# Prompt attention by head pairs, the SSD sample states and the sample outputs of cross attention as rows of adjacent products

## The chip, the cores and the metric

The kernel is one step of a hybrid streaming encoder and runs on one core of one Trainium2 chip. TensorE (PE) multiplies matrices and loads their stationary operands (PEld), VectorE (DVE), ScalarE (ACT) and GpSimd (POOL) do the elementwise work, and SyncE (SP) issues most loads. The metric is the device time of one execution in microseconds (us); smaller is better.

## The reference, cut to what matters

One layer computes, for a prompt of 512 tokens and for 8 sample streams of 16 tokens (one tile of 128 tokens), three branches, their merge, a cross attention and a feed-forward part. Three pieces matter here.

```python
def band_attn_prompt(q, k, v, rel_table):        # 8 heads of 64, chunks of 64 tokens
    ...
    s = einsum('bqhd,bkhd->bhqk', qb, kb) * 64 ** -0.5 + bias
    p = softmax(where(valid, s, neg))
    return einsum('bhqk,bkhd->bqhd', p, vb)

def ssd_chunk(h0, x, dt, bm, cm, a_neg):         # 16 heads of 64, 2 groups, state 128
    ...
    y_off = einsum('bign,bgrpn->bigrp', cm, h0g) * exp(ac)[..., None]
    h_new = h0g * exp(a_last)[..., None] + einsum('bjgn,bgrj,bjgrp->bgrpn', bm, exp(a_last - ac), xdt)
    ...

def memory_attn(h, mk, mv, wq, wo):              # 4 heads of 256 over 256 memory rows
    p = softmax(einsum('bqhd,bkhd->bhqk', q, mk) * 256 ** -0.5)
    o = einsum('bhqk,bkhd->bqhd', p, mv)
    return o @ wo
```

The prompt's attention has 4 query tiles of 128 tokens, and tile t sees t + 1 key tiles. For the samples, `y_off` and the cross attention read one state or one memory per stream, so their stationary operands are only 32 columns wide (two streams of 16 tokens, or 32 query columns of one head).

## The kernel before, in words

Everything is single precision. The large products (projections and feed-forward) split both operands into a high and a low part and run three products; the small products of attention and SSD run directly, and the compiler makes two TensorE instructions of each, so that one `mm` call stands as x2 in the profile.

The program is written by Python generators. Large products are "units" (`add`); each step of a unit is some 6 products. The steps of other work (attention, scans) yield a number, the amount of large products that `pump` puts behind that step, so that TensorE has something to do while VectorE and ScalarE work on the step. A tile scheduler then orders the instructions of each engine at build time, and each engine runs its own list strictly in order. PSUM has four buffers of 128x512 with the tag P for all small products (`PP`), and two double ones with the tag D for units (`PD`). Working tiles in SBUF come from a pool of 41 slots (`U`).

The stages that the change touches:

- `attn_prompt` (136 to 262 us in the profile). For 4 head pairs p, 4 query tiles t and 2 heads h: `scores` multiplies 64 rows of q with 64 rows of k (`asp`, half of the array's rows: rows 0 to 63 for the first head of a pair, 64 to 127 for the second), adds a bias, takes the row maximum and the softmax (`ae`). `out` transposes the probabilities (`apt`, copied to `apT`), and multiplies with the values (`apo`, 64 columns, half of the array's columns). The table `SKA = 3` keeps three heads' probabilities between `scores` and `out`.
- `ssd_sample` (680 to 722 and 840 to 882 us, once per group of 8 heads). For 4 pairs q of streams and 2 streams j: transpose the stream's state (`pht`, copied to `hT` by DVE for j = 0 and by ACT for j = 1), multiply with 32 columns of C (`pys`, a quarter of the array's columns, at columns 32 q), and update the state (`pcu`, then `sc` on DVE). The two `pys` tiles hold two of the four P buffers during the whole loop.
- `cross_sample` (1215 to 1312 us). For 8 streams b and 2 key tiles kt: the probabilities of 4 heads (32 columns each) times the stream's values (`xpv`, a quarter of the array's columns per head). The values come in two halves (`xcv`): heads 0 and 1 use the first, heads 2 and 3 the second.

The same scheduler puts other products between products that wait for different things. So the two halves of a stream's values lead to two pairs of `xpv` products with other work between them.

Of the kernel before, what the change touches and what calls it, by code (L numbers as in the profile page):

```python
# [11 lines left out]
ALU = mybir.AluOpType  # L12
# [7 lines left out]
NT = 5            # token tiles: 4 of the prompt, 1 with the 8 x 16 sample tokens  # L20
# [7 lines left out]
NGA, NGB, NGC = 5, 3, 5    # gates of the branches done ahead  # L28
# [4 lines left out]
SEQ = (0, 1, 2, 4, 3)   # tiles of a group's scan  # L33
LQ = 1
SKA = 3           # softmax tiles ahead of their products
MAGIC = float(0x5F3759DF)

NU = 41           # working slots of 128 x 640
NQ = 16           # of 128 x 128
NW = 6            # half weight tiles, and as many for the low parts  # L40
NS = 17           # small slots


class Enc:
# [39 lines left out]
    # Dense products come as units (generators that yield the time their products hold the tensor  # L84
    # engine); the steps of other work yield how much dense work is to be put behind them.
# [3 lines left out]
    def tick(self):  # L89
        """Next step of the work behind every finished product."""  # L90
        self.posts = [p for p in self.posts if next(p[1], self) is not self]
        for name in [n for n in self.ended if all(p[0] != n for p in self.posts)]:
            self.ended.remove(name)
            self.done.add(name)

    def post(self, gen):
        """First step of the work behind a product; the others come with later products."""
        if gen is not None and next(gen, self) is not self:
            self.posts.append((self.units[0][0] if self.units else None, gen))
# [34 lines left out]
    def weave(self, *gens, lead=0):  # L134
        """Steps of the generators in turn, the first one lead steps ahead."""
# [14 lines left out]
    def fmj(self, wk, X, post, m=P, c=0, nm="fm", split=False):  # L150
        """A weight-stationary product and the steps behind it."""
# [16 lines left out]
    def tmj(self, wk, X, cb, tiles=range(NT), nm="tm", t0=0, late=False):  # L168
        """cb(pair, ps[128 tokens, j, 256]): X^T (weights), per pair of token tiles; X starts at tile t0.
        late: the last row block comes after the others of the first two pairs."""  # L170
# [33 lines left out]
    def load2(self, out, in_):  # L204
        """A load that does not queue behind those of the weights."""
        self.nc.sync.dma_start(out, in_)

# [24 lines left out]
    def split(self, h, l, x, eng=None):  # L232
        """x = h + l exactly, both with 12 significant bits."""
        self.act(h, x)
        self.tt(l, x, h.bitcast(F32), ALU.subtract, eng)

    def rsqrt(self, v_in, scale, eps, post=1.0):
        """post / sqrt(v_in * scale + eps), elementwise on a small tile."""
# [18 lines left out]
    def sumsq(self, x, acc):  # L257
        """acc[p] = sum over the free axis of x*x."""
# [5 lines left out]
    def weights(self, w, c0, width, k0, nk, engs=None, loose=False):  # L264
        """Columns c0..c0+width of row blocks k0..k0+nk as [(h, l)] per row block."""
# [46 lines left out]
    def masks(self):  # L312
        nc = self.nc
        self.one = self.ones("one")
        self.mi = self.ones("mi")                             # [k, i] = 1 for k <= i
        self.keep(self.mi, [[1, P]], 0, -1)
        self.ms, blk = self.ones("ms"), self.Q("blk")         # [k, j] = 1 for k > j, within blocks of 16
# [7 lines left out]
        self.blkc = self.C("blkc", [P, 8])                    # [token, b] = 1 in block b  # L325
# [4 lines left out]
    def levels(self):  # L330
        """[j, i] = 1 where i lies in the upper half and j in the lower half of one block of 2s."""
        nc = self.nc
        self.par = self.C("par", [P, 2])                      # parity of the block of 16
        nc.vector.tensor_reduce(self.par, self.blkc.rearrange("p (a c) -> p c a", c=2), axis=AX.X, op=ALU.add)
        # packed: the diagonal blocks of 32 side by side
# [22 lines left out]
    def loads(self):  # L358
        """Loads of the small parameters and the convolutions' states."""
        I = self.I  # L360
        # vectors over features
# [14 lines left out]
        # parameters per head, on all partitions  # L376
# [16 lines left out]
    def params(self):  # L393
        nc = self.nc
        # vectors transposed; conv taps and gate gains come halved
# [35 lines left out]
    def rel_ap(self, h, nq, c0, n):  # L431
        """[nq, n]: bias of query q and key column c0 + c, column 128 being the query tile's first key."""
# [12 lines left out]
    def XT(self, nm):  # L445
        """Feature-major halves of all tokens: [(h, l)] per feature tile."""
# [3 lines left out]
    def token_norm(self, xs):  # L450
        """[128, n]: 1 / rms of the tokens of n tiles, each given as two halves."""
# [7 lines left out]
    def inv_rms(self, ss):  # L459
        """[128, n]: 1 / rms from the parts' sums of squares, [128, parts, n]."""  # L460
# [20 lines left out]
    def norm_tile(self, x, r, g):  # L481
        """Normalized halves of a token tile, transposed to psum: yields (j, psum [128, 4, 128])."""
# [8 lines left out]
    def norm_T(self, x, gain, to, groups=((0, 1), (2, 3), (4,))):  # L491
        """x[t]: two [128, 512] tiles; fills the feature-major halves of all tokens."""
# [63 lines left out]
    def store_conv(self, lt, cols, hist, op, os):  # L556
        """The batch's new states: row (f, token) of the prompt, then (f, stream, token)."""
# [12 lines left out]
    def decays(self, X):  # L570
# [4 lines left out]
        # 24 columns count, 8 more fill up a quarter of the array  # L575
        for c, c0, n in ((0, 3072, 8), (8, 6152, 16), (24, 3080, 8)):
            self.load(raw[:, :, c:c + n], wv[:, :, c0:c0 + n])
        # a quarter of the array for every two row blocks; their sums come with the transposes
# [15 lines left out]
    def decays_post(self, sb):  # L594
# [6 lines left out]
        # beta = sigmoid  # L601
# [3 lines left out]
        # softplus(x) = max(x, 0) + log1p(exp(-|x|)), log1p(e) = 2 atanh(e / (2 + e))  # L605
# [24 lines left out]
        # sums of the decays: up to a token, after a token, whole tile  # L630
# [27 lines left out]
        # the sums up to a token once more, a row per head, to be read by all partitions  # L658
# [6 lines left out]
    def decay(self, out, ts, hs, eng=None):  # L665
        """out[j, i], the sums of the decays up to token i for tiles ts or heads hs, become the decays from
        token j to i, where i >= j (and at most 1 elsewhere)."""
# [8 lines left out]
    def tr5(self, src, cols=None):  # L676
        """src(t) -> [128, 128]; returns two psum tiles, prompt [128, 512] and sample [128, 128]."""
# [7 lines left out]
    def gdn_dense(self, h, X):  # L685
# [7 lines left out]
        def post(kind):  # L693
            f = kind * 4 + h

            def run(ps):
                c = self.silu_conv(ps, "b", f, 3, [self.vc("bcw", i * 12 + f) for i in range(4)], None,
                                   (lt, kind, 3), "bc")
                if kind < 2:
                    # k and q stay as they are: what their l2 norms would scale goes by token  # L700
# [17 lines left out]
                if kind == 0:  # L718
# [3 lines left out]
                    self.stt(sc[:, 0, :], ss[:, NT:], EPS, rk, ALU.add, ALU.mult)       # 1 / rk  # L722
# [23 lines left out]
        for kind in (1, 0, 2):                                # k, q, v  # L746
            f = kind * 4 + h
            yield from self.fmj(lambda: self.weights(w, 1536 + f * P, P, 0, NK), X, post(kind), nm="bps")
        yield from self.fmj(lambda: self.weights(w, 3080 + h * P, P, 0, NK), X, gate, nm="gps")

    def gdn_solve(self, h):
        """Decays, both products with the keys, and the inverse of I + strictly upper part."""
# [11 lines left out]
        # decays between the tokens of a tile, [j, i]  # L764
# [28 lines left out]
        # E = (I + U)^-1 for U = strictly upper part, by doubling the block size; up to 32 on the diagonal  # L793
        # blocks alone, which lie packed side by side
# [24 lines left out]
        for i in range(1, 5):  # L819
            n = NT if i < 4 else 4                            # the sample's blocks are of 16 tokens  # L820
# [8 lines left out]
        # the blocks above the diagonal: -A^-1 B D^-1  # L829
# [34 lines left out]
    def gdn_run(self, h):  # L864
        """Per tile: w = E^T z, outputs and state; then norm over the head and gate."""
# [11 lines left out]
        # z = v - e^gc (k s0), w = E^T z, o = e^gc (q s0) + M^T w, state  # L877
# [60 lines left out]
        # norm over the head, gate, to feature-major halves  # L938
# [45 lines left out]
    def ssd_pre(self, g, t):  # L984
        """Decay matrices of 8 heads, [j, (h, i)], and the scaled inputs of a token tile."""
# [37 lines left out]
        if smp:  # L1023
            # inputs of the state's update in high and low parts, two streams' 32 tokens three times over:
            # (xh, xh, xl) and (bh, bl, bh), so that one pass brings all three products
# [68 lines left out]
    def ssd_sample(self, g, Cc, xs, bs, y, eg):  # L1094
# [5 lines left out]
        # decay of the whole block per (head, p) partition  # L1100
# [12 lines left out]
        pys = [self.PP("pys"), self.PP("pys")]  # L1113
# [6 lines left out]
        fetch(0)  # L1120
        for q in range(4):
# [3 lines left out]
            for j in range(2):  # L1125
# [6 lines left out]
                else:  # L1132
                    nc.vector.tensor_copy(hT, pt)
                yield FCS
# [801 lines left out]
```

## Time and profile before

| | |
|---|---|
| three runs, us | 1836.38, 1836.98, 1841.36 (median 1836.98) |
| span of the profiled execution, us | 1828.0 |
| PE busy | 1727.6 us, 95% of the span |
| DVE, ACT, POOL busy | 47%, 36%, 34% |
| chain of waits | PE 78%, DVE 10%, DMA 5%, ACT 3% |

The page gives no time of the profiled execution beside its span; the span is 9.0 us below the median of the runs. Busy time of PE is not a good measure of a product's cost, since products overlap in the array: the distance from the start of one row of the timeline to the start of the next is, as long as TensorE does not idle. The rows below are read that way.

### The profile page before, as it was taken

The numbers are of one execution on the slowest core, as the hardware profiler recorded it, in microseconds if no ns is written. First come the engines' busy times: TensorE is split into PE (matmuls) and PEld (weight loads), VectorE is DVE, ScalarE is ACT, GpSimd is POOL, SyncE is SP. The second block draws the span as 40 slices with busy tenths as digits, with TensorE's granted clock in tenths as the row PEclk, the third lists the DMA queues.
The fourth block names the chain that finished last, engine by engine and source line by source line (L and its number), as shares of the span: only waits on it lengthen the run. The fifth ranks groups of instructions, "written<-read, shape, count | busy, mean of one in ns | idle before, by whom it ended". The sixth has DMA issues, their size and how long they took to land.

```text
span 1828.0 us, 34046 instructions
## 1 busy us (share of the span) xinstructions
PE 1727.6 (95%) x13705; PEld 1593.3 (87%) x13705; DVE 866.0 (47%) x1778; ACT 652.7 (36%) x1611; POOL 612.5 (34%) x644
## 2 busy tenths in 40 slices
PE   6589999999999999999999899999989999999997
PEld 6587777889888887988989899987689999999997
DVE  5034655255777674665544463342474413431433
ACT  4034444432533442343342255332433312321333
POOL 4151222212332353453333236211144433433433
PEclk9889999999999999999999999999989999999999
DMA  5341127522221343234223435146332222222322
GB/s 156 64 113 54 49 70 243 184 67 61 78 76 52 98 121 115 72 110 133 78 68 92 138 126 164 58 162 230 105 93 82 70 71 81 75 66 70 93 77 76
DMA packets 239308, 182.41 MB, mean 100 GB/s; under 512 B 13313, under 2 KB 211982, under 8 KB 239150
## 3 DMA queue, kind: packets, MB, share of 16 engines
q1 hardware_dynamic: 216192, 164.69, 29.2%
q10 hardware_dynamic: 22958, 15.54, 3.3%
q8 instruction: 108, 1.77, 0.4%
q14 instruction: 50, 0.41, 0.1%
HBM read 162.04 MB, written 16.58 MB: 98 GB/s over the span
## 4 chain that ended last, share of the span: by engine, by line
PE 78%; DVE 10%; DMA 5%; ACT 3%; issue 2%; POOL 1%; ACTq 0%; SPq 0%; POOLq 0%; DVEq 0%
PE ups L210 8%; PE fps L210 8%; PE gps L210 8%; PE dn L210 8%; PE pps L210 6%; PE ap L210 6%; PE tm L210 4%; PE bps L210 4%; PE qps L210 3%; DMA raw<-in_w_in_dram 3%; PE cps L210 2%; PE aps L210 2%; DVE xc L221 2%; DVE t L218 1%; PE asp L210 1%
## 5 line engine op out<-in xcount | busy, mean ns | idle before, releaser
L218 POOL TENSOR_TENSOR wl<-raw,wh 128x512 fp32r<-128x512 f32 x376 | 494.5, 1323 | 1029.1 <-ACT wh L224 761.3
L224 ACT ACTIVATE wh<-raw 128x512 fp32r<-128x512 f32 x400 | 248.3, 629 | 606.2 <-PE dn L210 94.3
L210 PE MATMUL dn<-wh,hh 128*128 128x256 f32 x440 | 125.1, 284 | 0.4
L210 PE MATMUL dn<-wl,hh 128*128 128x256 f32 x440 | 124.7, 283 | 0.5 <-POOL wl L218 0.5
L210 PE MATMUL dn<-wh,hl 128*128 128x256 f32 x440 | 124.5, 283 | 0.0
L210 PE MATMUL gps<-xTh,wh 128*128 128x320 f32 x448 | 114.7, 333 | 1.8 <-DVE tg L221 1.8
L221 DVE SCALAR_TENSOR_TENSOR xc<-xp,vec,xc 128x664 f32<-128x664 f32 (+1 forms) x116 | 113.9, 982 | 3.1
L210 PE MATMUL gps<-xTl,wh 128*128 128x320 f32 x448 | 106.0, 314 | 0.0
L210 PE MATMUL gps<-xTh,wl 128*128 128x320 f32 x448 | 105.9, 314 | 0.0
L541 DVE TENSOR_SCALAR xc<-xp,vec 128x656 f32<-128x656 f32 (+1 forms) x34 | 32.2, 946 | 133.3 <-ACT xp L224 133.3
L210 PEld LDWEIGHTS dn<-wh,hh 128*128 128x128 f32 x440 | 84.4, 192 | 1.2 <-DVE x L218 1.0
L210 PEld LDWEIGHTS dn<-wl,hh 128*128 128x128 f32 x440 | 84.4, 192 | 0.9 <-POOL wl L218 0.9
L210 PEld LDWEIGHTS dn<-wh,hl 128*128 128x128 f32 x440 | 84.4, 192 | 0.0
L210 PEld LDWEIGHTS gps<-xTh,wh 128*128 128x128 f32 x448 | 72.9, 189 | 12.3 <-issue 9.1
L210 PE MATMUL fps<-fTh,wh 128*128 128x320 f32 x352 | 82.5, 312 | 0.0
L210 PE MATMUL fps<-fTl,wh 128*128 128x320 f32 x352 | 81.9, 310 | 0.0
L210 PE MATMUL ups<-fTh,wh 128*128 128x320 f32 x352 | 81.8, 310 | 0.0
L210 PE MATMUL fps<-fTh,wl 128*128 128x320 f32 x352 | 81.8, 310 | 0.0
L210 PE MATMUL ups<-fTh,wl 128*128 128x320 f32 x352 | 81.8, 310 | 0.0
L210 PE MATMUL ups<-fTl,wh 128*128 128x320 f32 x352 | 81.7, 310 | 0.0
L218 DVE TENSOR_TENSOR x<-x,dn 128x256 f32<-128x256 f32 x60 | 23.0, 418 | 118.5 <-PE dn L210 118.5
L210 PEld LDWEIGHTS gps<-xTh,wl 128*128 128x128 f32 x448 | 75.3, 189 | 1.7 <-issue 1.7
(517 smaller groups left out, 4620.3 us busy)
## 6 DMA issues: line engine op xcount, KB each, us to landing
raw<-in_w_in_dram SPq DMA_DIRECT2D x72, 512.0 KB
raw<-in_w_up_dram SPq DMA_DIRECT2D x44, 512.0 KB
raw<-in_w_down_dram SPq DMA_DIRECT2D x20, 512.0 KB
ck<-in_cache_attn_k_dram SPq DMA_DIRECT2D x32, 256.0 KB
cv<-in_cache_attn_v_dram SPq DMA_DIRECT2D x32, 256.0 KB
xck<-in_cache_mem_k_dram SPq DMA_DIRECT2D x32, 256.0 KB
xcv<-in_cache_mem_v_dram SPq DMA_DIRECT2D x32, 256.0 KB
raw<-in_wx_o_dram SPq DMA_DIRECT2D x14, 512.0 KB
```

The costliest lines, as they stand in the source:

```text
L210: self.nc.tensor.matmul(out, lhsT=lhsT, rhs=rhs, start=start, stop=stop)
L218: return (eng or self.nc.vector).tensor_tensor(out, a, b, op=op)
L221: self.nc.vector.scalar_tensor_tensor(out, a, s, b, op0=op0, op1=op1)
L224: self.nc.scalar.activation(out, in_, f, **kw)
L541: nc.vector.tensor_scalar(acc[:, :n], xp[:, :n], taps[0], bias, op0=ALU.mult, op1=ALU.add)
```

## The change

Three functions issue their narrow products in another order. Comments and docstrings were also taken out, which changes line numbers alone.

`attn_prompt`: `scores` takes a head pair and issues both heads' `asp` products one behind the other, then both softmaxes. `out` transposes both heads, then issues the `apo` products of both heads in turn, key tile by key tile, and copies the result once. `SKA` now counts pairs.

`ssd_sample`: the eight `hT` tiles are kept, and the `pys` products come behind the loop, four in a row for each j; the `pys` buffers are taken only then, and each row of four is followed by one more yield.

`cross_sample`: the four heads are taken in the order 2, 3, 0, 1.

```diff
-SKA = 3           # softmax tiles ahead of their products
+SKA = 1
...
-        pys = [self.PP("pys"), self.PP("pys")]
...
+        hTs = [[], []]
         for q in range(4):
...
+                hTs[j].append(hT)
                 yield FCS
-                self.mm(pys[j][32 * q:32 * q + 32, :], Cc[:, 512 + 32 * q:512 + 32 * q + 32], hT)
...
+        pys = []
+        for j in range(2):
+            pys.append(self.PP("pys"))
+            for q in (3, 0, 1, 2):
+                self.mm(pys[j][32 * q:32 * q + 32, :], Cc[:, 512 + 32 * q:512 + 32 * q + 32], hTs[j][q])
+            yield FCS
...
-        def scores(p, t, h):
+        def scores(p, t):
...
-            r = slice(64 * h, 64 * h + 64)
-            sp = self.PP("asp")
-            self.mm(sp[:, :n], q[r, t * P:(t + 1) * P], k[r, :n])
...
+            sps = [self.PP("asp") for _ in range(2)]
+            for h in range(2):
+                r = slice(64 * h, 64 * h + 64)
+                self.mm(sps[h][:, :n], q[r, t * P:(t + 1) * P], k[r, :n])
...
-            for kt in range(t + 1):
-                self.mm(po[r, :P], V[kt][:, p * P + 64 * h:p * P + 64 * h + 64], pT[:, kt * P:(kt + 1) * P],
-                        start=(kt == 0), stop=(kt == t))
-            if h:
-                self.act(self.YA[p][:, t * P:(t + 1) * P], po[:, :P])
...
+                pTs.append(pT)
+                yield FA * (t + 1)
+            po = self.PP("apo")
             for kt in range(t + 1):
+                for h, pT in enumerate(pTs):
+                    self.mm(po[64 * h:64 * h + 64, :P], V[kt][:, p * P + 64 * h:p * P + 64 * h + 64],
+                            pT[:, kt * P:(kt + 1) * P], start=(kt == 0), stop=(kt == t))
+            self.act(self.YA[p][:, t * P:(t + 1) * P], po[:, :P])
...
-                for h in range(2):
-                    pend.append((p, t, h, scores(p, t, h)))
-                    yield FA * (t + 1)
+                pend.append((p, t, scores(p, t)))
+                yield 2 * FA * (t + 1)
...
-                for h in range(4):
+                for h in (2, 3, 0, 1):
                     self.mm(pv[32 * h:32 * h + 32, :256], pT[:, kt * P + 32 * h:kt * P + 32 * h + 32],
```

On TensorE in the prompt's attention, head pair 0, where the products of query tile 1 (`apo`) and the scores of query tile 3 (`asp` 128x512) stand, before:

```order
L210 MATMUL apo_1390<-apT_1388,V_341 64x128
L210 MATMUL apo_1390<-apT_1388,V_342 64x128
L210 MATMUL asp_1393<-aqk_739,aqk_676 128x512
L215 MATMUL apt_1431<-ident,ae_1307 128x128 x2
L215 MATMUL t5a_1436<-ident,aqk_1171 128x128 x4
L215 MATMUL t5b_1437<-ident,aqk_1171 128x128
L210 MATMUL aps_1452<-xTh_134,wl_1456 128x320
L210 MATMUL apo_1390<-apT_1434,V_341 64x128
L210 MATMUL apo_1390<-apT_1434,V_342 64x128
L210 MATMUL asp_1481<-aqk_739,aqk_676 128x512
```

and now:

```order
L210 MATMUL apo_1401<-apT_1388,V_341 64x128
L210 MATMUL apo_1401<-apT_1393,V_341 64x128
L210 MATMUL apo_1401<-apT_1388,V_342 64x128
L210 MATMUL apo_1401<-apT_1393,V_342 64x128
L210 MATMUL asp_1407<-aqk_739,aqk_676 128x512
L210 MATMUL asp_1408<-aqk_739,aqk_676 128x512
L215 MATMUL t5a_1437<-ident,aqk_1171 128x128 x4
L215 MATMUL t5b_1438<-ident,aqk_1171 128x128
```

Both heads' products now alternate, and both heads' scores are neighbours. Of the 16 pairs of scores, 14 stand so; two have something between them (pair 2, tile 2: large products; pair 3, tile 3: three `apo`). Of the 16 groups of `apo`, three are cut into two pieces.

On TensorE at the end of the second group's sample states (`tm` are the large products of the output gate), before:

```order
L210 MATMUL pys_9761<-hT_10098,cc_9055 32x512
L215 MATMUL pht_10119<-ident,sc_9988 128x128 x4
L210 MATMUL pcu_10132<-bs_9575,xs_9569 128x256 x2
L210 MATMUL tm_10202<-wh_10184,xTh_134 128x256
L210 MATMUL tm_10202<-wh_10184,xTl_136 128x256
L210 MATMUL tm_10202<-wl_10185,xTh_134 128x256
L210 MATMUL tm_10202<-wh_10184,xTh_134 128x256
L210 MATMUL tm_10202<-wh_10184,xTl_136 128x256
L210 MATMUL pys_9762<-hT_10124,cc_9055 32x512
L210 MATMUL pcu_10139<-bs_9575,xs_9569 128x256 x2
```

and now:

```order
L210 MATMUL tm_10076<-wh_9905,xTl_137 128x256
L210 MATMUL tm_10076<-wl_9906,xTh_135 128x256
L210 MATMUL pys_10138<-hT_10090,cc_9055 32x512
L210 MATMUL pys_10138<-hT_9774,cc_9055 32x512
L210 MATMUL pys_10138<-hT_9870,cc_9055 32x512
L210 MATMUL pys_10138<-hT_9990,cc_9055 32x512
L210 MATMUL pys_10143<-hT_10109,cc_9055 32x512
L210 MATMUL pys_10143<-hT_9793,cc_9055 32x512
L210 MATMUL pys_10143<-hT_9921,cc_9055 32x512
L210 MATMUL pys_10143<-hT_10017,cc_9055 32x512
L210 MATMUL py_10154<-xdt_9688,dx_9657 128x64 x4
L210 MATMUL py_10154<-xdt_9688,dx_9659 128x64 x4
```

Here both rows of four adjoin; in the first group 12 large products stand between them. From the first `pht` to the last `pcu` of this group stand 135 large products now, and 164 before; in the first group it is 145 and 149.

On TensorE in cross attention, stream 0, key tile 0 (`xkt` transposes the next stream's keys), before:

```order
L210 MATMUL xpv_13881<-xcv_13882,ypT_13856 32x256 x2
L215 MATMUL xkt_13906<-ident,xck_13772 128x128
L215 MATMUL xkt_13906<-ident,xck_13776 128x128
L210 MATMUL xpv_13881<-xcv_13883,ypT_13856 32x256 x2
L215 MATMUL xkt_13906<-ident,xck_13772 128x128
L215 MATMUL xkt_13906<-ident,xck_13776 128x128
```

and now:

```order
L210 MATMUL ap_13959<-wh_13789,oxl_12869 128x256
L210 MATMUL ap_13959<-wl_13790,oxh_12867 128x256
L210 MATMUL xpv_13881<-xcv_13883,ypT_13856 32x256 x2
L210 MATMUL xpv_13881<-xcv_13882,ypT_13856 32x256 x2
L215 MATMUL xkt_13906<-ident,xck_13772 128x128
L215 MATMUL xkt_13906<-ident,xck_13776 128x128
```

The four heads are one row in all 16 places, and 5 to 10 more large products stand ahead of the first row of an even stream.

## Rows read from the trace of the kernel before

**Rows 1.** The page's chain of waits: shares of the span by engine.

```profile
PE 78%; DVE 10%; DMA 5%; ACT 3%; issue 2%; POOL 1%; ACTq 0%; SPq 0%; POOLq 0%; DVEq 0%
```

**Rows 2.** Windows by stage: us, busy PE, PEld, DVE, ACT, POOL; clock, DMA share, GB/s.

```profile
137.00:262.00 125.00, 124.41 (x809) 96.66 (x808) 69.75 (x243) 54.78 (x172) 30.98 (x51) 1.00 0.18 51
...
840.00:882.00 42.00, 40.74 (x283) 32.87 (x284) 26.92 (x59) 15.34 (x43) 11.78 (x10) 1.00 0.41 121
1215.00:1312.00 97.00, 96.92 (x752) 68.95 (x752) 30.11 (x68) 25.52 (x59) 11.60 (x9) 1.00 0.52 180
```

**Rows 3.** PE timeline, one pair of `xpv`: start us, length us, instruction, count.

```profile
1226.99 0.28 PE L210 MATMUL ap<-wh,oxl 128*128 128x256 f32 x1
1227.11 0.28 PE L210 MATMUL ap<-wl,oxh 128*128 128x256 f32 x1
1227.32 0.63 PE L210 MATMUL xpv<-xcv,ypT 128*32 128x256 f32 x4
1227.87 0.44 PE L215 MATMUL xkt<-ident,xck 128*128 128x128 f32 x2
```

**Rows 4.** PE timeline, one `pys` alone.

```profile
685.29 1.05 PE L210 MATMUL pys<-hT,cc 128*32 128x512 f32 x2
686.27 0.55 PE L215 MATMUL pht<-ident,sc 128*128 128x128 f32 x3
```

**Rows 5.** PE timeline, four quarter-array products of `pys`'s shape in a row.

```profile
352.49 1.06 PE L210 MATMUL ssp<-skT,qbd 128*32 128x512 f32 x8
353.49 0.41 PE L210 MATMUL gps<-xTh,wh 128*128 128x320 f32 x1
```

**Rows 6.** PE groups by form: `xpv` and `pys`, count, busy us, mean ns.

```profile
L210 PE MATMUL xpv<-xcv,ypT 128*32 128x256 f32 x128 | 20.0, 391 | 0.0
L210 PE MATMUL pys<-hT,cc 128*32 128x512 f32 x32 | 16.7, 604 | 1.6 <-DVE hT L1133 1.1 <-ACT hT L224 0.5
```

**Rows 7.** PE timeline, single `asp` of query tiles 0 and 3.

```profile
162.24 0.48 PE L210 MATMUL asp<-aqk,aqk 64*128 64x128 f32 x2
162.66 0.55 PE L215 MATMUL apt<-ident,ae 128*128 128x128 f32 x3
...
178.90 1.12 PE L210 MATMUL asp<-aqk,aqk 64*128 64x512 f32 x2
179.95 0.42 PE L210 MATMUL bps<-xTh,wl 128*128 128x320 f32 x1
```

**Rows 8.** PE timeline, both heads' `asp` of tile 0, then one of tile 1.

```profile
139.65 0.97 PE L210 MATMUL asp<-aqk,aqk 64*128 64x128 f32 x6
140.54 0.56 PE L210 MATMUL aps<-xTh,wl 128*128 128x320 f32 x2
```

**Rows 9.** PE timeline, one head's `apo` of tiles 3 and 0.

```profile
165.00 1.09 PE L210 MATMUL apo<-apT,V 128*64 128x128 f32 x8
166.02 0.70 PE L210 MATMUL asp<-aqk,aqk 64*128 64x256 f32 x2
...
172.41 0.43 PE L210 MATMUL apo<-apT,V 128*64 128x128 f32 x2
172.77 0.91 PE L210 MATMUL asp<-aqk,aqk 64*128 64x384 f32 x2
```

**Rows 10.** Tile `apT`: DVE's copies of transposed probabilities, ns min/median/max, times, forms.

```profile
L1343 DVE COPY apT<-apt x16: 274/486/693, 145.7 to 255.1; 128x128 f32<-128x128 f32 x4, 128x256 f32<-128x256 f32 x4, 128x384 f32<-128x384 f32 x4, 128x512 f32<-128x512 f32 x4
```

**Rows 11.** DVE timeline, softmax of one head of tile 3.

```profile
180.06 0.69 DVE L1326 CUSTOM_DVE_ANT_0 ae<-asp,bias 128x512 f32<-128x512 f32 x1 [1.34 <-PE asp L210]
...
182.09 0.49 DVE L1300 TENSOR_SCALAR ae<-ae,ers 128x512 f32<-128x512 f32 x1
```

**Rows 12.** The tile `xcv`: idle time of PEld before its loads, ended by that DMA.

```profile
  DMA xcv<-in_cache_mem_v_dram: 0.7, 4
```

**Rows 13.** SP timeline: issue of one stream's four value loads.

```profile
1220.93 2.35 SPq L206 DMA_DIRECT2D xcv<-in_cache_mem_v_dram  x4
```

**Rows 14.** PE timeline, second pair of `xpv` of the same stream.

```profile
1228.24 0.63 PE L210 MATMUL xpv<-xcv,ypT 128*32 128x256 f32 x4
```

More of the change, by code (lines that the diff above doesn't have):

```diff
@@ L1315, in attn_prompt @@
         V = self.V
-        pos = {}
-        def scores(p, t, h):
+        def scores(p, t):
             q, k = self.QK[p]
             n = P * (t + 1)
-            r = slice(64 * h, 64 * h + 64)
-            sp = self.PP("asp")
-            self.mm(sp[:, :n], q[r, t * P:(t + 1) * P], k[r, :n])
-            e = self.U("ae", shape=(P, 512))
-            mx = self.SM("amx", [P, 1])
-            nc.vector.tensor_tensor_reduce(out=e[:, :n], in0=sp[:, :n], in1=bias[p][h][:, 512 - n:], scale=1.0,
-                                           scalar=NEG, op0=ALU.add, op1=ALU.max, accum_out=mx)
-            nm = self.SM("anm", [P, 1])
-            nc.vector.tensor_single_scalar(nm, mx, -1.0, op=ALU.mult)
-            self.softmax(e[:, :n], n, nm)
-            return e
@@ L1333, in out @@
-        def out(p, t, h, e):
-            n = P * (t + 1)
-            r = slice(64 * h, 64 * h + 64)
-            pt = self.PP("apt")
-            for kt in range(t + 1):
-                self.tr(pt[:, kt * P:(kt + 1) * P], e[:, kt * P:(kt + 1) * P])
-            pT = self.U("apT", shape=(P, 512))
-            if h:
-                self.act(pT[:, :n], pt[:, :n])
-            else:
-                nc.vector.tensor_copy(pT[:, :n], pt[:, :n])
-                pos[0] = self.PP("apo")
-            yield FA * (t + 1)
-            po = pos[0]
-            for kt in range(t + 1):
-                self.mm(po[r, :P], V[kt][:, p * P + 64 * h:p * P + 64 * h + 64], pT[:, kt * P:(kt + 1) * P],
-                        start=(kt == 0), stop=(kt == t))
-            if h:
-                self.act(self.YA[p][:, t * P:(t + 1) * P], po[:, :P])
+            sps = [self.PP("asp") for _ in range(2)]
@@ new lines, in scores @@
+            for h in range(2):
+                r = slice(64 * h, 64 * h + 64)
+                self.mm(sps[h][:, :n], q[r, t * P:(t + 1) * P], k[r, :n])
+            es = []
+            for h, sp in enumerate(sps):
+                e = self.U("ae", shape=(P, 512))
+                mx = self.SM("amx", [P, 1])
+                nc.vector.tensor_tensor_reduce(out=e[:, :n], in0=sp[:, :n], in1=bias[p][h][:, 512 - n:], scale=1.0,
+                                               scalar=NEG, op0=ALU.add, op1=ALU.max, accum_out=mx)
+                nm = self.SM("anm", [P, 1])
+                nc.vector.tensor_single_scalar(nm, mx, -1.0, op=ALU.mult)
+                self.softmax(e[:, :n], n, nm)
+                es.append(e)
@@ new lines, in scores, with out @@
+            return es
+        def out(p, t, es):
+            n = P * (t + 1)
+            pTs = []
+            for h, e in enumerate(es):
+                pt = self.PP("apt")
+                for kt in range(t + 1):
+                    self.tr(pt[:, kt * P:(kt + 1) * P], e[:, kt * P:(kt + 1) * P])
+                pT = self.U("apT", shape=(P, 512))
+                if h:
+                    self.act(pT[:, :n], pt[:, :n])
+                else:
+                    nc.vector.tensor_copy(pT[:, :n], pt[:, :n])
+                pTs.append(pT)
+                yield FA * (t + 1)
+            po = self.PP("apo")
+            for kt in range(t + 1):
+                for h, pT in enumerate(pTs):
+                    self.mm(po[64 * h:64 * h + 64, :P], V[kt][:, p * P + 64 * h:p * P + 64 * h + 64],
+                            pT[:, kt * P:(kt + 1) * P], start=(kt == 0), stop=(kt == t))
+            self.act(self.YA[p][:, t * P:(t + 1) * P], po[:, :P])
@@ L1359, in attn_prompt @@
                     bias[p + 1] = self.prompt_bias(p + 1)
-                for h in range(2):
-                    pend.append((p, t, h, scores(p, t, h)))
-                    yield FA * (t + 1)
-                    if len(pend) > SKA:
-                        yield from out(*pend.pop(0))
+                pend.append((p, t, scores(p, t)))
+                yield 2 * FA * (t + 1)
+                if len(pend) > SKA:
+                    yield from out(*pend.pop(0))
             bias.pop(p - 1, None)
```

## The prediction

> **What bounds the kernel now.** I read the chain of waits first [rows 1]: 78% of what sets the end is PE, and DVE, DMA and ACT together have 18%. Then the windows of the stages that the change touches [rows 2]: PE is busy 124.41 of 125 us in the prompt's attention, 40.74 of 42 in the second group's sample states, 96.92 of 97 in cross attention, and the granted clock is 1.00 (2.4 GHz) in all of them. There PE is what the time is made of, and a slot of PE that goes is time that goes, until another engine comes late. DVE is next, with 69.75 of 125 and 26.92 of 42. Last the timeline of PE, read from the start of one row to the start of the next, which I call a slot.
>
> One thing about slots comes first. A product of another array shape costs the product ahead of it something: from `ap` to `ap` is 0.12 us, from `ap` to the first `xpv` 0.21 [rows 3]. So each change into a narrow row costs 0.09.
>
> **Cross attention.** A pair of `xpv` holds PE for 0.55 (1227.32 to 1227.87), with the change of shape 0.64 [rows 3]. There are 128 instructions [rows 6], four to a pair: 32 pairs, 20.5 us. Now 16 rows of four. What four cost is seen in another product: `ssp`, the same quarter of the array with 512 columns, takes 1.00 for a whole row of four [rows 5], while `pys` takes 0.98 for one alone [rows 4]. Four cost what one costs. With 256 columns that is (1.00 - 0.09) / 2 + 0.09 = 0.55, the pair's slot; 16 x 0.64 = 10.2. Removed: **10.2 us**.
>
> What it adds is a wait: the row starts when the later of the two halves of the values is there, since heads 2 and 3 come first. Behind it in PE's queue stand the `xkt` transposes and all large products. The four loads of one stream are issued from 1220.93 on, over 2.35 us [rows 13]; the pair on the first half starts at 1227.32 [rows 3], the one on the last half at 1228.24 [rows 14], and all waits for `xcv` come to 0.7 us in 4 places [rows 12]. The row starts where the first pair stood, so the last half is needed 0.92 earlier. The bounds are 0 (it had landed, and 5 to 10 more large products stand ahead of the even streams' first rows) and 5 (0.92 less some slack, in 8 streams, with 0.7 already there). I take 1.7, nearest to the measured 0.7.
>
> **SSD's sample states.** `pys` has 32 instructions, two to a product [rows 6]: 16 products at 0.98 [rows 4] and 0.09, 17.1 us. Now four rows of 1.00 [rows 5], two of them adjoining, so three changes of shape: 4.3. Removed: **12.8 us**. PE also waited 1.6 us for `hT` just ahead of `pys` [rows 6]; behind the loop all copies but the last are old, so I add 1.6. Against it stands the cover. From the first `pht` to the last `pcu` the order has 145 large products instead of 149 in the first group, next to nothing, but 135 instead of 164 in the second. Those 29 products, 0.12 each [rows 3], are not lost, but 3.5 us of cover over DVE's chain is. DVE has 26.92 us of work in those 42 [rows 2]; a loop of some 32 us has about 0.64 of that share, 20.5 us, and shrinks by 8 x 1.07 for `pys` and by 3.5 to 20, so DVE could come to bound it. The bounds are 0 (slack takes it) and 7 (it is late by twice that). I take the whole 3.5. Net of the waits: -1.9.
>
> **The prompt's attention: scores.** One head's `asp` holds PE for 0.42 at tile 0 (162.24 to 162.66) and 1.05 at tile 3 (178.90 to 179.95) [rows 7]; between them it grows by 0.21 a tile, 0.42 + 0.63 + 0.84 + 1.05 = 2.94 for four tiles, 11.8 for four pairs of one head. Do two halves of the rows overlap? Before, the first two heads of tile 0 happen to stand together, with one of tile 1: six instructions in 0.89 (139.65 to 140.54) [rows 8], where 0.42 + 0.42 + 0.63 would be 1.47. They do. So a pair takes one head's time: 11.8 are removed, less the pair that stood together already (0.42) and the two that the order still separates (0.84 and 1.05), 9.5, and 13 changes of shape, 1.2. Removed: **10.7 us**.
>
> **The prompt's attention: outputs.** One head's `apo` takes 1.02 at tile 3 and 0.36 at tile 0 [rows 9], 0.22 a tile, 0.36 + 0.58 + 0.80 + 1.02 = 2.76, 11.0 for one head of all pairs, and 16 changes of shape, 1.4. The order cuts three groups after the first product (overlap lost 0.36, 0.29 and 0.27, some change of shape): 1.1. Removed: **11.4 us**, if halves of the columns overlap as quarters do [rows 5]. No row has two such halves together; the bounds are 0 and 11.4.
>
> What it adds: `apo` of a pair waits for the copies of both heads, the second of them just ahead. A copy takes 0.27 to 0.69, median 0.49 [rows 10]; 16 of them bare would be 8, with their last transposes 10, and none is 0, since each is followed by some large products. Before, single heads waited in the same way, so I take 2. One pair ahead instead of three heads gives the softmax less time: one head of tile 3 takes from 180.06 to 182.58 on DVE [rows 11], and PE has about 5 to 6 us between a pair's scores and its transposes (the products that the order puts there, at the slots above). Two heads in turn share DVE but fit, so nothing is taken for that here.
>
> **The sum.** 10.2 + 12.8 + 10.7 + 11.4 = 45.1; less 1.7 + 1.9 + 2 = 5.6, it is 39.5. The profiled execution's span is 1828.0, and 1828.0 - 39.5 = 1788.5. The page has no time of that execution beside its span; the median of the runs, 1836.98, lies 9.0 above it. 1788.5 + 9.0 = 1797.5, and I say **1797**.
>
> One rule speaks against the sum. The Trainium skill, "TensorE: Matmul & The Clock Gate", "Part 3: Packing small matmuls — row/col tiling", says that a weight load overlaps running products only if its group of rows differs. By it, column neighbours would not overlap, and `xpv`, `pys` and `apo` would gain little. For quarters the trace disagrees: eight instructions on quarters of columns in 1.00 us [rows 5]. For halves no row here shows it.
>
> **Rivals.**
>
> *Column halves don't overlap.* Then `apo` saves only its changes of shape, 1.4, and the rest of 11.4 stays: 1797 + 10 = 1807. For it: no row shows halves of 64 columns side by side, and each has its own weights to load. Against it: quarters do overlap, in pairs and in fours [rows 3, 5]. Chance 0.07. That rule of the skill points here.
>
> *Softmax comes late.* A pair's scores now end together, so the second head's softmax starts behind the first's on DVE: two times 0.69 and 0.49 and small ones, with ACT's exponentials between [rows 11], some 4 us from the scores to the last probability. If large products and a former pair's `apo` give less cover than that, PE stands at `apt`, and what packing saved is waited for. DVE's work stays, 69.75 us in what would be 103 [rows 2]: 0.68, so not its rate but its latency would decide. If it eats all of this stage's 22, the time is 1797 + 20 to 22, some 1818. Against it: 5 to 6 us of products stand there by the order. Chance 0.10.
>
> The skill's "TensorEngine Tiling (Array Packing)", "PSUM Bottleneck", says the same in general: tiling speeds up TensorE but not the emptying of PSUM, which may then bound. The trace's 0.68 is below that point.
>
> *Slower: rows of four wait for the values.* In cross attention PE's queue stops until the last half has landed. A half's loads are issued 5 to 7 us before their first use [rows 13, 14]; were each of 16 rows to wait 7 us, 112 would be added to 1797, some 1909. It decides from 45.1 / 16 = 2.8 us a row on, where all is given back. Against it: waits of 0.7 in 4 places in all [rows 12], and DMA at 0.52 [rows 2]. Chance 0.03.
>
> **How the numbers follow.** Forecast 0.80, column halves 0.07, late softmax 0.10, late values 0.03. Nothing lost at all would be 1837 - 45.1 = 1792, with the 1.6 of `hT` 1790, and a little more if freed PSUM buffers help: low end **1787**. The high end is about half of the gain lost, or the softmax case nearly whole: **1815**. A measurement of this kernel can tell 0.3%, 5.5 us, from no change: below 1831.5 is faster. The first three cases are, but for mixtures of several: faster 0.94, within 0.3% 0.03, slower 0.03.
>
> **What would show it.** Rows of `xpv` of eight instructions in about 0.55 us; rows of `pys` of eight in 1.0; both heads' `asp` of tile 3 in 1.05; sixteen `apo` of tile 3 in about 1.0, and not 2.0. The attention's stage 125 to about 105, sample states 42 to about 35 and 37, cross attention 97 to about 89. Idle PE ahead of `apt`, `apo`, `pcu` or `xpv` of over 10 us in all would make it wrong, and so would `apo` rows as long as two heads'.

## The result and the profile after

The changed kernel takes 1812.87 us (median of 4 runs, 1809.45 to 1814.71) against 1836.99; the ratio is 0.9867 with an interval of 0.9847 to 0.9886. That is 24.1 us less. The forecast was 1797, 39.5 less; 1812.87 lies near the upper end of its range. All four sorts of rows take the slots that were forecast. What was not foreseen is how long PE stands idle between them, and the low clock behind that.

The span of the profiled execution is 1807.7 us, its own time 1809.45. PE's share of the chain falls from 78 to 69% [rows 1]:

```profile
PE 69%; DVE 10%; DMA 3%; ACT 3%; issue 2%; POOL 1%; ACTq 0%; POOLq 0%; SPq 0%; DVEq 0%
```

The rows themselves, on PE's timeline of the changed kernel (start, length, instruction, count). `xpv`, one stream [rows 3, 14]:

```profile
1219.11 0.64 PE L210 MATMUL xpv<-xcv,ypT 128*32 128x256 f32 x8
1219.68 1.20 PE L215 MATMUL xkt<-ident,xck 128*128 128x128 f32 x9
```

`pys` of the first group [rows 4]:

```profile
710.52 1.06 PE L210 MATMUL pys<-hT,cc 128*32 128x512 f32 x8
711.52 0.56 PE L210 MATMUL pps<-yh,wh 128*128 128x320 f32 x2
...
713.47 1.06 PE L210 MATMUL pys<-hT,cc 128*32 128x512 f32 x8
714.46 0.56 PE L210 MATMUL pps<-yh,wh 128*128 128x320 f32 x2
```

Both heads' `asp` and `apo` of tile 3 [rows 7, 9]:

```profile
153.90 1.13 PE L210 MATMUL asp<-aqk,aqk 64*128 64x512 f32 x4
154.96 0.65 PE L215 MATMUL t5a<-ident,aqk 128*128 128x128 f32 x4
...
165.58 1.09 PE L210 MATMUL apo<-apT,V 128*64 128x128 f32 x16
166.60 0.70 PE L210 MATMUL asp<-aqk,aqk 64*128 64x256 f32 x4
```

Start to start, eight instructions of `xpv` hold PE for 0.57, eight of `pys` for 1.00, four of `asp` for 1.06, sixteen of `apo` for 1.02: what two, one, one head and one head took before.

Then the waits. PE's idle time ahead of `apo`, by what ended it (us, times), first in the kernel before and then in the changed one:

```profile
  DVE apT L1343: 0.5, 1
```

```profile
  DVE apT L1355: 5.0, 6
  ACT apT L224: 0.3, 1
```

The waits that stand out on PE's timeline, in the attention, the first and the second SSD group:

```profile
192.13 1.10 PE L210 MATMUL apo<-apT,V 128*64 128x128 f32 x12 [2.41 <-DVE apT L1355]
...
692.38 0.66 PE L215 MATMUL pht<-ident,sc 128*128 128x128 f32 x2 [4.11 <-DMA sc<-in_state_c_ssm_dram]
...
858.08 0.62 PE L210 MATMUL pcu<-bs,xs 96*128 96x256 f32 x2 [1.31 <-DVE sc L221]
860.00 0.58 PE L210 MATMUL tm<-wh,xTh 128*128 128x256 f32 x1 [1.30 <-DVE zt L221]
```

And the windows behind two of them, with the columns of [rows 2]. The third column from the right is the granted clock:

```profile
192.00:194.00 2.00, 1.87 (x17) 1.32 (x18) 1.51 (x3) 0.77 (x4) 1.74 (x3) 0.66 0.00 0
194.00:196.00 2.00, 2.00 (x10) 2.00 (x11) 2.00 (x6) 0.37 (x2) 0.00 (x0) 0.50 0.77 191
196.00:198.00 2.00, 2.00 (x15) 2.00 (x14) 1.97 (x10) 1.10 (x5) 0.10 (x1) 0.99 0.66 202
...
692.40:698.00 5.60, 5.60 (x23) 5.56 (x24) 0.00 (x0) 0.70 (x1) 0.00 (x0) 0.52 0.36 101
698.00:704.00 6.00, 6.00 (x44) 6.00 (x44) 2.25 (x8) 1.26 (x2) 1.33 (x2) 1.00 0.40 119
```

After 2.41 us without a product the clock is at its lower level, 1.2 GHz (0.50), for some 3.4 us, and 1.7 us are lost. After 4.11 us it is low for the next 5.6, 0.48 x 5.6 = 2.7 lost. In the prompt's attention and in both SSD groups of the kernel before, it was 1.00 throughout.

To see where the time went I took the same instruction in both traces and followed how much earlier it starts. The idle time is the sum of the gaps over 0.06 us in which no product is in flight; the cost of the clock is one less the granted clock, times the length, while PE works; slots are what is left, so they hold the errors of the others too. Each stretch ends where the same products stand at a fixed distance in both traces.

| stretch of before, us | forecast | measured | idle | clock | slots |
|---|---|---|---|---|---|
| 0 to 140, not changed | 0 | +2.6 | | | |
| 140 to 330, prompt's attention and what follows | -20.1 | -9.9 | +8.1 | +1.7 | -19.7 |
| 678 to 735 and 838 to 888, SSD | -10.9 | -2.8 | +5.2 | +5.5 | -13.4 |
| 1212 to 1355, cross attention and what follows | -8.5 | -11.3 | +2.2 | -2.6 | -10.8 |
| all between | 0 | +1.1 | | | |
| sum | -39.5 | -20.3 | | | |

The clock's -2.6 stands behind the cross attention's stage, where the kernel before ran at the lower level for 17.1 us from 1323 us on and the changed one for 10.2; that this follows from the change is not shown. The profiled executions differ by 20.3 and the medians by 24.1; the reason for the difference is below.

### The profile page after: what moved, and what is told of

It reads as the page before. It is cut to its first block, busy times and chain, and to the rows that moved or that the text cites. A ratio compares the mean times of both kernels' runs of the same rounds, so it can differ in the third digit from the quotient of the medians.

```text
span 1807.7 us, 34056 instructions
## 1 busy us (share of the span) xinstructions
PE 1691.8 (94%) x13705; PEld 1585.8 (88%) x13705; DVE 862.5 (48%) x1778; ACT 652.3 (36%) x1611; POOL 613.3 (34%) x644
## 4 chain that ended last, share of the span: by engine, by line
PE 69%; DVE 10%; DMA 3%; ACT 3%; issue 2%; POOL 1%; ACTq 0%; POOLq 0%; SPq 0%; DVEq 0%
PE ups L210 9%; PE fps L210 8%; PE gps L210 8%; PE dn L210 8%; PE pps L210 6%; PE ap L210 5%; PE tm L210 4%; PE qps L210 3%; PE cps L210 2%; DVE xc L221 2%; PE bps L210 2%; PE pl L210 1%; DVE t L218 1%; PE py L210 1%; DMA raw<-in_wx_v_dram 1%
```

## The experiments

**e1, the attention alone.** `ssd_sample` and `cross_sample` as before.

> Only the prompt's attention is changed; SSD and cross attention are as before. My theory (slots came out as forecast, cover did not): both heads' products save about 21 us of PE slots, about 9 us of new idle time ahead of apo and apt and about 2 us of low clock take half of it back, so the stage from 140 to 323 us ends about 10 us earlier, and the whole is 8 to 12 us below the kernel before. Rival (the stage loses through what the other two parts do to loads and slots): the stage saves 18 us or more alone.

1826.57 us, ratio 0.9939 (0.9917 to 0.9961), 11 us faster. PE is idle for 6.4 us in the stage (before 0.6), 5.6 of it ahead of `apo`, and the stretch from 140 to 330 us gains 9.8 by its trace, as in the changed kernel. So the stage loses this part of its gain by itself, and the rival falls.

**e2, SSD alone.** `attn_prompt` (with `SKA = 3`) and `cross_sample` as before.

> Only SSD's sample states are changed. My theory (eight kept hT tiles hold working slots, so the state loads sc are issued late): the wait of about 4 us for sc in the first group and a fall of the clock behind it are there also with the attention as before; the two groups save 1 to 5 us in all, where the slots say 13. Rival (the loads were late because the attention ahead was shorter): no wait for sc over 1 us, and 9 us or more saved.

1832.66, ratio 0.998 (0.9962 to 0.9998), 5 us faster at the medians; by its trace the two SSD stretches gain 1.7. The wait is there, with the attention of before, on PE's timeline:

```profile
708.71 0.66 PE L215 MATMUL pht<-ident,sc 128*128 128x128 f32 x2 [4.14 <-DMA sc<-in_state_c_ssm_dram]
```

The rival falls: SSD makes it by its own order. That says nothing yet of the kept tiles.

**e3, cross attention alone.** `attn_prompt` (with `SKA = 3`) and `ssd_sample` as before.

> Only the order of heads in cross attention is changed. My theory: 16 rows of four instead of 32 pairs save 10 us of slots, the wait for the values' last half is about 1 us, so 9 to 12 us below the kernel before. Rival (rows of four wait for values, and the gain of this stage in the changed kernel was the clock): under 6 us.

1830.93, ratio 0.996 (0.9943 to 0.9977), 6.7 faster: between the two. By its trace the stage itself starts 7.8 us later and ends 2.1 earlier than in the trace of before, 9.8 saved, about what the rows say; the later start comes from the stretch ahead, which this kernel doesn't change.

**e4, rows of two in SSD**, the rest as changed:

```
-        pys = []
-        for j in range(2):
-            pys.append(self.PP("pys"))
-            for q in (3, 0, 1, 2):
...
+            if q % 2:                       # within the loop over q
+                if q == 1:
+                    pys = [self.PP("pys"), self.PP("pys")]
+                for j in range(2):
+                    for qq in (q, q - 1):
+                        self.mm(pys[j][32 * qq:32 * qq + 32, :], Cc[...], hTs[j][qq])
+                yield FCS
```

> The changed kernel, with pys in rows of two after every second pair of streams: four hT tiles are kept and not eight. Slots: 8 rows of 1.0 us and 4 changes of shape instead of 4 rows and 3, about 4.1 us more than the changed kernel. My theory (kept tiles starve the state loads): the wait for sc of 4.1 us and the low clock behind it (2.7 us) go, and part of the second group's idle time, so it is 2 to 7 us faster than the changed kernel. Rival (the waits have another cause, such as the cover that is missing in the loop): 3 to 5 us slower than the changed kernel.

1806.91, ratio 0.9834 (0.9807 to 0.9861): 6 us below the changed kernel at the medians, with 4 us more slots; by the traces the two SSD stretches gain 4.4 on it. No wait that the profile ties to `sc` is left. It fits the kept tiles, but it fits the missing cover too: two rows of `pys` and large products now stand between the second and the third pair of streams again.

**e8, slots held.** As e1, and in the loop six tiles taken and held:

```
                 hT = self.U("hT", shape=(P, 512))
+                if q < 3:
+                    hold.append(self.U("hold", shape=(P, 512)))
+                    nc.gpsimd.memset(hold[-1][:, :1], 0.0)
...
+        for t in hold:
+            self.tt(y[:, :1], y[:, :1], t[:, :1], ALU.add, nc.gpsimd)
```

> As e1 (attention alone changed, pys single within the loop), but six working slots are taken one by one where the first six hT tiles are made, and held to the end of the loop; nothing else is changed but six tiny writes and reads on GpSimd. My theory (kept tiles starve the state loads): without any row of pys, PE waits 3 us or more for sc in the first group, with a fall of the clock behind it, and the time is 3 to 9 us above e1. Rival (it was the missing cover in the loop, not the slots): no wait for sc over 1 us and the time of e1 within 2 us.

1828.52, ratio 0.9947 (0.993 to 0.9964), that of e1 within 2 us, and no wait for `sc` at all. Kept tiles alone don't make it: my theory fell, and its rival, the missing cover, is left standing. What is different in the changed kernel besides is SyncE's own list. Its timeline there (SPq: issue, with the time an issue took):

```profile
681.84 0.37 SPq L206 DMA_DIRECT2D sc<-in_state_c_ssm_dram  x1
685.91 0.37 SPq L227 DMA_DIRECT2D raw<-in_w_in_dram  x1
686.37 0.53 SPq L206 DMA_DIRECT2D sc<-in_state_c_ssm_dram  x1
690.02 0.37 SPq L227 DMA_DIRECT2D raw<-in_w_in_dram  x1
690.70 10.06 SPq L206 DMA_DIRECT2D sc<-in_state_c_ssm_dram  x2
```

in the kernel before and in e8, where two weight loads stand ahead of all four:

```profile
694.19 3.80 SPq L227 DMA_DIRECT2D raw<-in_w_in_dram  x2
700.04 9.55 SPq L206 DMA_DIRECT2D sc<-in_state_c_ssm_dram  x4
...
690.34 3.81 SPq L227 DMA_DIRECT2D raw<-in_w_in_dram  x2
696.62 9.88 SPq L206 DMA_DIRECT2D sc<-in_state_c_ssm_dram  x4
```

and in e4, which has no wait:

```profile
684.98 0.37 SPq L206 DMA_DIRECT2D sc<-in_state_c_ssm_dram  x1
689.03 0.37 SPq L227 DMA_DIRECT2D raw<-in_w_in_dram  x1
689.50 4.83 SPq L206 DMA_DIRECT2D sc<-in_state_c_ssm_dram  x3
```

In the changed kernel the scheduler put a weight load between the two state loads of the third pair of streams. It went out at 685.91, and the second state load right behind it at 686.37; its transposes began at 692.38, 6.0 later. In e8 and in the kernel before, PE's transposes on that load began 2.5 us after it went out, without a wait. But e4 has the same weight load in the same place. There the transposes on the second load came 7.0 us after it went out; in the changed kernel PE was ready for them after 1.9 (692.38 - 4.11 = 688.27). So the wait needs both: a load that goes out late behind the weight load, and a PE that comes early because no `pys` and fewer large products stand ahead of the third pair.

**e9, states two pairs ahead**, all else as changed:

```
         fetch(0)
+        fetch(1)
...
-            if q < 3:
-                fetch(q + 1)
+            if q < 2:
+                fetch(q + 2)
```

> The changed kernel (rows of four), with the states of the first two pairs of streams loaded ahead of the loop and the others two pairs ahead, so that in SyncE's list both loads of the third pair stand ahead of the weight load between them. e8 took slots away and no wait came, so my first theory has fallen. New theory (the second load of the third pair stands in SyncE's queue behind a weight load that waits for a free weight tile): the 4.1 us ahead of pht and the low clock behind it go, 4 to 8 us faster than the changed kernel. Rival (the loads wait for working slots all the same, with eight kept tiles more than in e8): sc is issued no earlier than at 684 us, a wait for sc or for weights of over 2 us stays, and the time is that of the changed kernel within 3 us.

1809.88, ratio 0.985 (0.9831 to 0.9868): 3.0 faster at the medians, short of the 4 to 8, and the interval overlaps that of the changed kernel, so the time alone shows no gain. SyncE's timeline:

```profile
676.12 0.37 SPq L227 DMA_DIRECT2D raw<-in_w_br_b_dram  x1
678.27 2.09 SPq L206 DMA_DIRECT2D sc<-in_state_c_ssm_dram  x2
688.51 0.37 SPq L227 DMA_DIRECT2D raw<-in_w_in_dram  x1
```

Both loads of the third pair go out by 680 and the wait is gone; the clock stays at 1.00 there, and between 680 and 720 us of before the kernel gains 6.0 on the changed one. That is the forecast's size (4.1 + 2.7). It then loses 2.4 of that between 838 and 888 us of before: PE now waits 1.2 us for `hT` at the start of the second group and 0.5 ahead of the next `pht`, and the clock falls behind it, 1.7 lost. So by the trace the theory holds for the first group: the earlier load, now 10.7 us ahead of its transposes, removes the wait. The second group has a wait of its own, most of it on DVE.

**e5, `apo` one step later** (on e4):

```
-                yield FA * (t + 1)
-            po = self.PP("apo")
+                yield FA * (t + 1)
+            late.append((p, t, pTs))
+
+        def outV(p, t, pTs):
+            po = self.PP("apo")
...
+                if late:
+                    outV(*late.pop(0))
                 if len(pend) > SKA:
-                    yield from out(*pend.pop(0))
+                    yield from outT(*pend.pop(0))
```

> As e4 (rows of two in SSD), and a pair's apo products stand one step later, behind the next pair's scores, so that one step of large products lies between the copies apT and apo. My theory (in the attention PE waits for the copies apT, which stand in DVE's queue behind the convolutions and softmaxes of others; 5 us, and 2 us of low clock behind the longest): idle time ahead of apo falls under 1.5 us, and it is 4 to 8 us faster than e4. Rival (the softmax itself is late, so the wait moves to apt): idle time ahead of apt and apo together stays over 5 us and the time is that of e4 within 2 us.

1805.48, ratio 0.9833 (0.9808 to 0.9859). The idle time ahead of `apo`, first in e5, then as it was in e4:

```profile
  ACT xp L224: 1.3, 1
```

```profile
  DVE apT L1356: 5.0, 6
  ACT apT L224: 0.3, 1
```

The wait for copies is gone, as expected, and not moved to `apt` (0.2). All idle time from 142 to 256 us falls from 6.9 to 3.3, and the stretch from 140 to 330 us of before gains 4.4 on e4. The time falls by 1.4 at the medians, not by the 4 to 8 of the forecast, and by 5.1 between the profiled executions; the medians alone can't tell it from none.

**e6, two pairs ahead** (`SKA = 2` on e4).

> As e4, with two pairs of scores ahead instead of one (SKA 2). Rival (softmax with one pair ahead is late): idle time in the attention falls by over 5 us, 5 to 8 us faster than e4. My theory (the copies are late, not the softmax): the 0.8 us ahead of apt go, the waits ahead of apo stay, within 2 us of e4.

1809.46, ratio 0.9861 (0.9838 to 0.9885), no faster than e4: 2.6 slower at the medians, with intervals that overlap. The wait ahead of `apt` goes (0.9 to 0), that ahead of `apo` falls from 5.3 to 4.5 only. All idle time of the stage falls from 6.9 to 4.5. So a late softmax is a smaller part of it, and the late copies the larger.

**e7, both copies on ScalarE** (on e4).

```
-                if h:
-                    self.act(pT[:, :n], pt[:, :n])
-                else:
-                    nc.vector.tensor_copy(pT[:, :n], pt[:, :n])
+                self.act(pT[:, :n], pt[:, :n])
```

> As e4, with both heads' copies apT on ScalarE. My theory (DVE's queue ahead of the copy makes the wait): waits ahead of apo for DVE go from 5.0 us to none, those for ACT come to 1 to 3 us, as the two copies now stand one behind the other on an engine with 53 us of work in the stage; 1 to 5 us faster than e4. Rival (it is the transposes that are late, whichever engine copies): as much idle time ahead of apo as in e4, 5 us or more, within 1 us of e4 or slower.

1812.3, ratio 0.9866 (0.9842 to 0.989): 5.4 slower than e4, a miss. Ahead of `apo`:

```profile
  ACT apT L224: 6.6, 6
```

It isn't DVE's list alone. ScalarE's list has other work ahead of the copies too, and that work waits for DVE in its turn. Ahead of the longest of these waits, 2.25 us:

```profile
195.77 0.83 ACT L224 ACTIVATE bc<-xc 128x512 f32<-128x512 f32 x2 [4.01 <-DVE xc L221]
196.50 0.61 ACT L224 ACTIVATE wh<-raw 128x512 fp32r<-128x512 f32 x1
197.02 0.85 ACT L224 ACTIVATE apT<-apt 128x384 f32<-128x384 f32 x2
```

ScalarE stood idle for 4 us behind a convolution of DVE (`xc`), with the copies behind that in its list. As both heads' copies now follow one another on one engine, e7 doesn't tell how much each part costs. The wait disappeared where more stood between copy and product (e5). Two of these waits are over 2 us, and the clock falls behind both; the stretch from 140 to 330 us loses 7.2 on e4, 6.5 of it clock.

**e10, e5 with the states two pairs ahead.**

> e5 (rows of two in SSD, apo one step later) with the states loaded two pairs ahead as in e9. Rows of two have no wait for sc left to remove; new theory: within 2 us of e5. Rival (states late cost something there too): 2 us faster or more.

1809.78, ratio 0.9857 (0.9837 to 0.9878), 4.3 above e5 at the medians, slower than both expected, though the intervals overlap. With rows of two no wait for `sc` was left to remove, and PE now waits 1.6 us for `hT` in the first group and 3.2 in the second, for `hT` and `zt`. From 890 to 1130 us, which the edit doesn't touch, low clock costs 10.2 us instead of the 6.8 of e5 (one less the granted clock, times the length); whether that follows from the edit is open. Ahead of the second group's last `pht` PE waits 1.7 us, here as in e4, e5 and e6, and the profile ties that to nothing.

**e11, rows of four with both mended.**

> e9 with apo one step later as in e5: both mended, all rows of four kept. If the new theory and the one on the copies hold, the gains add up: 8 to 13 us faster than the changed kernel, about 1800 to 1805, and 1 to 4 us below e5, since rows of four save 4 us more slots than rows of two. Rival (kept tiles or the missing cover cost more than the 4 us in any case): e5 or slower.

1804.8 (1799.0 to 1805.59), ratio 0.9812 (0.9792 to 0.9832): 8.1 below the changed kernel, with intervals apart, and the lowest median of all. From e5 it isn't told apart (0.7 at the medians). Of the second group's waits, DVE's 1.31 and 1.30 are as in the changed kernel.

## Why the prediction was right in part

**The slots: right.** The forecast had 45.1 us of slots, 22.1 in the attention, 12.8 in SSD, 10.2 in cross attention. Measured by the table it is 19.7, 13.4 and 10.8, in sum 44.0. The argument from the start-to-start distance of the nearest row of the same shape held, and so did the step to halves of the columns, for which there was no row: sixteen `apo` in 1.02. The first rival falls: sixteen `apo` took 1.02, not 2.0. The Trainium skill, "TensorE: Matmul & The Clock Gate", "Part 3: Packing small matmuls — row/col tiling", says that a weight load overlaps running products only if its group of rows differs. The traces disagree: the eight weight loads of a row of `pys`, all of 128 rows, stand in the first 0.16 us of that row (710.52 to 710.68 on PEld), while its first products run. That column neighbours would gain little was my inference from this sentence alone; a table of the same section of the Trainium skill gives 2.38 times the speed for three column tiles.

So the miss is in the waits and behind them. In the three stretches PE's idle time grew by 15.5 us, where 5.6 were deducted, and the clock cost 4.6, where nothing was: 44.0 - 15.5 - 4.6 = 23.9, close to the 24.1 of the medians. The prediction's own sign of being wrong, over 10 us of idle time ahead of `apt`, `apo`, `pcu` or `xpv`, was all but met: 1.1 + 5.5 + 1.6 + 1.2 = 9.4 (gaps over 0.06 us), and the 4.1 ahead of `pht` was not on that list.

**"so I take 2": too small.** The wait of `apo` for the copies was priced at 2 with an upper bound of 10, by the waits of single heads before. It measured 5.3, and all idle time of the stage grew by 6.4 (0.6 to 6.9). The failing step is "Before, single heads waited in the same way", with the cover of "each is followed by some large products". Large products did follow. But the copies came later than before: of the 32, 19 started within 0.1 us of their last transpose in the trace of before, and 1 in that after; on average DVE's copies started 2.4 us behind it instead of 1.1, ScalarE's 1.6 instead of 0.4. Ahead of the longest wait, 2.41 us, PE and then DVE:

```profile
181.72 0.49 PE L215 MATMUL apt<-ident,ae 128*128 128x128 f32 x3
182.93 0.49 PE L215 MATMUL apt<-ident,ae 128*128 128x128 f32 x3
...
186.18 3.83 DVE L221 SCALAR_TENSOR_TENSOR xc<-xp,vec,xc 128x664 f32<-128x664 f32 x3
190.12 0.18 DVE L527 COPY xp<-st_b 128x24 f32<-128x24 f32 x1
190.71 0.90 DVE L221 SCALAR_TENSOR_TENSOR bc<-bc,xc 128x512 f32<-128x512 f32 x2 [0.41 <-ACT bc L224]
191.52 0.55 DVE L1355 COPY apT<-apt 128x384 f32<-128x384 f32 x1
```

Behind the pair's last transposes PE had 6.3 us of large products, but the first head's copy stood in DVE's list behind a convolution and started 9.3 us after its transposes. With a further step ahead of `apo` the waits for the copies go (e5). By e6 the softmax is the smaller part, and by e7 another engine's list does no better. Why the lists came out in this order is not shown. So the second rival, the late softmax, named the right stage and half of the price, and mostly the wrong place in the chain.

**SSD's waits: the wrong ones.** I took 3.5 for missing cover in the second group and gave 1.6 back for `hT`. The second group did wait, 2.7 more, on DVE (`sc`, `zt`), as forecast. But the first group's largest wait, 4.1 for a state load, was in no term: the prediction looked at the place of large products and of copies, not at what SyncE's list has between a pair's two loads. The cover that it called "next to nothing" in the first group (145 large products instead of 149) left out where they stand, and the `pys` that left the loop. e2 shows that the edit makes the wait by itself, e8 that slots held do not, e9 that moving the load ahead of the weight load removes it, and e4 that with rows of two the same place of the weight load costs nothing. Why the scheduler placed the weight load there is not shown.

**The clock: left out.** The sum treated an idle microsecond as one microsecond. Behind the waits above the clock fell, and that cost 1.7 + 5.5 = 7.2 us more (4.6 with the -2.6 behind cross attention), above the whole deduction of 5.6.

**"lies 9.0 above it": an accident of one execution.** For the changed kernel each run's time lies some 1.8 above its span (1809.45 and 1807.7; 1812.16 and 1810.4). So the profiled execution of before took some 1829.8, an estimate, 7.2 us less than the median of its kernel, and runs of the same kernel later went from 1830.65 to 1844.19. Adding 9.0 was right for the median, but the span to subtract from was that of a lucky execution: in its trace the first 140 us, which nothing changes, are 2.6 us shorter than after, and the clock fell nowhere in the stages of the change. The changed kernel's profiled execution was 3.4 below its own median. 7.2 - 3.4 = 3.8 is the difference between the 24.1 of the medians and the 20.3 of the traces.

**The third rival falls.** Cross attention waited for its values once, 1.2 us (2.6 in e4), and its stretch gained 11.3, 2.6 of it by the clock.

## What to carry to other kernels

Narrow products that lie side by side in the array and stand in a row cost one of them here, and that can be read beforehand from any row of the same shape; what can't be read from PE's rows is which list the next operand now waits in, so follow each operand of a bunched row back through its copy's engine and through the queue of its load. The work between a copy and its consumer has to cover what stands ahead of the copy in its engine's list too, whichever engine makes it. Price a wait with the clock that falls behind it, and before adding a difference between a span and a median, compare one run's span with its own time.

## What the runs showed of the hardware

The same wait doesn't always bring a fall of the clock. PE's wait for `gr`, a tile that DVE makes, ahead of the first SSD group was 1.87 us in the trace of before, 1.87 in e8 and 2.03 in e4; in the first the clock stayed at 1.00 behind it, in e8 1.7 us were lost (windows of 2 us, one less the granted clock), in e4 3.4. Runs of one kernel that differ by several us may well differ by such falls; that was not tested by itself.
